# A third quarter of a down projection's columns in seven products of half size

## The chip, the cores and the metric

The kernel runs on one core of a Trainium2 chip. The metric is the device time of one execution in microseconds (us). TensorE (PE) multiplies, VectorE (DVE) and ScalarE (ACT) work elementwise, GpSimd (POOL) and SyncE (SP) here issue transfers: SP the plain loads of weights, POOL the loads that are to be added to what already lies on the chip.

## The reference

A decoder trunk of two layers over 256 tokens and 2048 features, in float32. What the change touches is the MLP, which stands in both layers:

```python
def sq_relu_mlp(u, w_up, w_down):
    hid = jax.nn.relu(u @ w_up)
    return (hid * hid) @ w_down
```

`w_up` is 2048 x 8192, `w_down` 8192 x 2048. Around it stand a mixer (linear attention in layer 0, forgetting attention in layer 1), an embedding gate and norms.

## The kernel before, in words

**Three products for one.** Every float32 weight is split into a high part of reduced precision (`whi`, cast by ACT) and the rest (`wlo`, subtracted by DVE); activations are split the same way. A product is then three matmuls: high x high, high x low, low x high. One split works on 128 x 1024 values and fills one *pair* of buffers (`whi`, `wlo`). There are four pairs, taken in turn, and three `raw` buffers of 128 x 2048 into which SP loads. ACT casts a pair as soon as TensorE has left the pair four before it; DVE follows ACT.

**The MLP.** The 8192 hidden features are worked through in eight blocks of 1024. For block b, eight `up` pieces (128 hidden features each) compute `hid`: weights are the stationary operand, the 256 tokens of `u_m` are streamed, 48 matmuls of 256 columns for two pairs. In between, the pieces of the down projection for block b-1 run with `hid` as the stationary operand (128 tokens) and the weights streamed; they are written out as a list of names that is walked in order (`for item in "up up p1 p2 n0 ..."`). `Line` ties every matmul of the MLP to the one before it, so TensorE runs the pieces exactly in the order of that list. For DVE, ACT and the queues the framework's scheduler chooses the order.

**The down projection before.** The last block (b = 7) goes another way and is not touched. For blocks 0 to 6 of each layer the 2048 output columns are cut in two:

- Columns 0 to 1023 by seven products of half size in place of eight (the scheme of Winograd and Strassen: two halves of the tokens, two of the block's features, two of the columns). The pieces are `p1` to `p7`, 12 matmuls of 512 columns each, in a PSUM bank `pp` that `into` adds to an accumulator `acc1` to `acc7` in SBUF. Five of the seven need sums of weights. They come about in two buffers, `cA` and `cB` (`chain`): POOL loads one quarter of the weights, and once a piece has split it, loads the next quarter with an adding transfer (`accum_op`). The sums of activations (`form`) are made by DVE (line L312).
- Columns 1024 to 2047 plainly, in four pieces `n0` to `n3` of 24 matmuls of 512 columns, which add up over all blocks in four PSUM banks `pn`.

`mm_tokens` (the mixers' values, `pst`) also streams weights past stationary activations: 512 columns in layer 0 (`u_a`), 416 in layer 1 (`u_kv`).

**Where operands start.** Activation buffers start some floats into their tiles: `u_a`, `u_kv` and others at 60 (28 in slot C); `hid` at 36 (4 in slot C), 24 less; weights at 0.

Of the kernel before, what the change touches and what calls it, by code (L numbers as in the profile page):

```python
# [18 lines left out]
P = 128  # L19
# [16 lines left out]
def yoco_kernel(ctx, tc, a, out):  # L36
# [53 lines left out]
    def load_slab(src, n, parts, before=None):  # L90

        raw = wp.tile([P, D], F32, name="raw", tag="raw", bufs=3)
        m = n // parts
        if not before:
            nc.sync.dma_start(raw[:, :n], src)
        got = []
        for i in range(parts):
            r = raw[:, i * m : (i + 1) * m]
            if before:
                before[i]()  # L100
                nc.sync.dma_start(r, src[:, i * m : (i + 1) * m])
            got.append(split(r, m))
        return got

    def split(r, m, to=None, **dims):
        hi = wp.tile([P, 1024], F32R, name="whi", tag="whi", bufs=4)
        lo = wp.tile([P, 1024], F32R, name="wlo", tag="wlo", bufs=4)
        h_, l_ = (x[:, :m].rearrange(to, **dims) if to else x[:, :m] for x in (hi, lo))
        nc.scalar.copy(h_, r)  # L109
        nc.vector.tensor_tensor(l_, r, h_.bitcast(F32), op=ALU.subtract)  # L110
        return hi, lo
# [32 lines left out]
    def mm_tokens(src, act, cols, before=None, after=None):  # L144
# [22 lines left out]
    class Stats:  # L167
# [18 lines left out]
        def rstd(self):  # L186
# [4 lines left out]
            r = base.tile([P, T], F32, name="rstd", tag="rstd", bufs=1)  # L191
# [54 lines left out]
    def mlp(layer, u, stats, slots, u2, g2, pool, pps):  # L246
# [10 lines left out]

        nonlocal h
# [8 lines left out]
        def quarter(b, q, n):  # L267

            return wd[b // 2, b % 2, q, :, 4 * n : 4 * n + 4, :]

        def load(eng, dst, src, **kw):
            eng.dma_start(dst.rearrange("p (n f) -> p n f", n=4), src, **kw)  # L272
        acc = {}
        nsum = None
# [42 lines left out]
        def product(o, op, pairs, start, stop=True):  # L317

            for j in range(4):
                hi, lo = (w[:, j % 2 * 512 : (j % 2 + 1) * 512] for w in pairs[j // 2])  # L320
# [5 lines left out]
        def into(name, ps):  # L326

            if name not in acc:
                acc[name] = pool.tile([P, 512], F32, name="acc" + name, tag="acc" + name, bufs=1)
# [5 lines left out]
        nbank = [[pps.tile([P, 512], F32, name=f"pn{c}{t}", tag=f"pn{c}{t}") for t in range(2)] for c in range(2)]  # L335
# [5 lines left out]

        def loaded(src):
            raw = wp.tile([P, D], F32, name="raw", tag="raw", bufs=3)
# [3 lines left out]
        def down(b):  # L347
# [9 lines left out]
            def one(name, op, pairs):  # L357
                o = psm.tile([P, 512], F32, name="pp", tag="mm")
                product(o, op, pairs, True)
                into(name, o)  # L360

            def p1():
                load(nc.gpsimd, cA, quarter(b, 0, 0))
                pairs = halves(cA)
                load(nc.gpsimd, cA, quarter(b, 0, 1), accum_op=ALU.add)
                one("1", plain(0, 0), pairs)

            def p2():

                load(nc.gpsimd, cB, quarter(b, 1, 1))  # L370
# [7 lines left out]
            def p3():  # L378
                pairs = halves(cB)
                load(nc.gpsimd, cB, quarter(b, 0, 1), accum_op=ALU.add)  # L380
                one("3", form(3), pairs)

            def p6():
                pairs = halves(cA)
                load(nc.gpsimd, cA, quarter(b, 1, 0), accum_op=ALU.add)
                one("6", form(1), pairs)

            def p7():
                one("7", form(2), halves(cB))
# [4 lines left out]
            def n(c, q):  # L394

                pairs = loaded(quarter(b, q, 2 + c))
                for t in range(2):
                    product(nbank[c][t], plain(q, t), pairs, b == q == 0, b == NBL - 2 and q == 1)

            return dict(p1=p1, p2=p2, p3=p3, p4=p4, p5=p5, p6=p6, p7=p7,  # L400
                        n0=lambda: n(0, 0), n1=lambda: n(0, 1), n2=lambda: n(1, 0), n3=lambda: n(1, 1))
# [14 lines left out]
        for to, of, op in ("21+", "61-", "46-", "47-", "56+", "35+", "75+"):  # L416
            nc.vector.tensor_tensor(acc[to], acc[to], acc[of], op=ALU.add if op == "+" else ALU.subtract)
        nsum = pool.tile([P, 4, 512], F32, name="nsum", tag="nsum", bufs=1)
        for i in range(4):
            nc.scalar.copy(nsum[:, i], nbank[i // 2][i % 2])  # L420
        sums = [(acc["2"], acc["4"]), (acc["3"], acc["7"]), (nsum[:, 0], nsum[:, 1]), (nsum[:, 2], nsum[:, 3])]
# [5 lines left out]
        def back(m):  # L427

            for i in range(2):
                n = 4 * m + 2 * i  # L430
                ptr = pps.tile([P, 2, T], F32, name="ptr", tag=f"pn{m % 2}{i}")
                for j in range(2):
                    for t in range(2):
                        nc.tensor.transpose(ptr[:, j, t * P : (t + 1) * P], sums[m][t][:, (n + j) % 4 * P : ((n + j) % 4 + 1) * P], ident)  # L434
# [23 lines left out]
    def ple(layer, u, stats, pt, after, pool, pps):  # L458
# [6 lines left out]
        for n in range(KC):  # L465
            if n % 8 == 0:
                wu = load_slab(a["w_pu"][layer, n // 8], D, 2)
                if n == 0:
                    ups = [two(i) for i in "1562"]
                else:  # L470
                    more = pool.tile([P, 4, 2, T], F32, name="ups", tag="nsum", bufs=1)
                    ups = [more[:, i] for i in range(4)]
                for i in range(4):
                    pu = pps.tile([P, 2, T], F32, name="pu", tag=f"pn{i // 2}{i % 2}")
# [332 lines left out]
    with tc.tile_pool(name="at", bufs=2) as ap, tc.tile_pool(name="aps", bufs=1, space=PSUM) as aps:  # L807
# [30 lines left out]
        nd = ap.tile([NH, T], F32, name="nd", bufs=1)  # L838
# [173 lines left out]
```

## Time and profile before

| | |
|---|---|
| median of 3 runs | 2445.43 us (2445.01 to 2446.1) |
| the profiled execution | 2444.84 us, its span 2443.1 us |
| granted TensorE clock, mean | 0.997 |
| busy: PE / DVE / ACT / POOL | 99% / 72% / 58% / 5% |
| one block of the MLP (640 to 724 us): PE / DVE / ACT busy | 84.0 / 61.5 / 47.1 us |

A matmul's duration in the profile runs to the end of its pipeline, so that neighbours overlap. What one costs in a dense row is the length of the row over its count; the chain in order of time shows such rows.

### The profile page before, as it was taken

How to read it: one execution, taken by the hardware profiler on the slowest of the kernel's cores; microseconds unless marked ns; L12 is line 12 of the kernel's file. 1: busy time of each engine (PE TensorE's matmuls, PEld its weight loads, DVE VectorE, ACT ScalarE, POOL GpSimd, SP SyncE). 2: the span in 40 equal slices, each digit the busy share in tenths (PEclk: the TensorE clock that was granted, in tenths of full speed). 3: DMA queues.
4: the chain of work that ended last, by engine and by line, in shares of the span. 5: the costliest groups of instructions: out<-in, count | busy, mean ns of one | idle time of the engine just before them, and what ended most of it. 6: DMA issues, size and time to landing. Idle time of an engine off the chain costs nothing.

```text
span 2443.1 us, 43577 instructions
## 1 busy us (share of the span) xinstructions
PE 2427.9 (99%) x18024; PEld 2307.7 (94%) x18024; DVE 1765.2 (72%) x2738; ACT 1411.9 (58%) x2112; POOL 119.2 (5%) x159
## 2 busy tenths in 40 slices
PE   9999999999999999999999999999999999999998
PEld 8999999999999999999999999999999999999997
DVE  7797797676777777778874566667677777776876
ACT  7666575565555555555754545556555555555664
POOL 1000000000000000000000000000000000000000
PEclk9999999999999999999999999999999999999999
DMA  6455555578878887876555655557887888778653
GB/s 246 172 182 187 181 174 191 213 259 234 227 234 235 251 237 237 235 223 225 188 178 188 197 177 182 171 196 261 239 231 236 240 245 230 244 231 233 218 190 121
DMA packets 129270, 521.72 MB, mean 214 GB/s; under 512 B 8688, under 2 KB 9264, under 8 KB 91696
## 3 DMA queue, kind: packets, MB, share of 16 engines
q1 hardware_dynamic: 88256, 415.66, 47.8%
q0 software_dynamic: 39520, 101.25, 19.4%
q8 instruction: 141, 2.31, 0.4%
q10 hardware_dynamic: 1296, 2.03, 0.2%
q14 instruction: 57, 0.47, 0.1%
HBM read 512.58 MB, written 6.32 MB: 212 GB/s over the span
## 4 chain that ended last, share of the span: by engine, by line
PE 99%; DVE 0%; ACT 0%; DMA 0%; issue 0%; ACTq 0%; DVEq 0%
PE ps L127 29%; PE pn L127 12%; PE ps L141 12%; PE ps L139 12%; PE ps L140 12%; PE pp L127 11%; PE pst L127 7%; PE pu L141 0%; PE pu L139 0%; PE pu L140 0%; PE pa L671 0%; PE ptr L434 0%; PE pl L874 0%; PE ptp L897 0%; DVE h L945 0%; DMA raw<-in_w_av 0%
## 5 line engine op out<-in xcount | busy, mean ns | idle before, releaser
L110 DVE TENSOR_TENSOR wlo<-raw,whi 128x1024 fp32r<-128x1024 f32 (+2 forms) x798 | 964.8, 1210 | 382.9 <-ACT whi L109 369.8
L109 ACT CAST whi<-raw 128x1024 fp32r<-128x1024 f32 (+2 forms) x798 | 830.8, 1042 | 661.1 <-PE ps L140 281.6
L127 PE MATMUL ps<-u_m,whi 128*128 128x256 f32 x4096 | 701.8, 276 | 0.0
L127 PEld LDWEIGHTS ps<-u_m,whi 128*128 128x128 f32 x4096 | 621.6, 188 | 4.3
L127 PE MATMUL ps<-u_m,wlo 128*128 128x256 f32 x2048 | 564.7, 276 | 0.0
L127 PEld LDWEIGHTS ps<-u_m,wlo 128*128 128x128 f32 x2048 | 384.7, 188 | 0.0
L109 ACT CAST whi<-chain 128x1024 fp32r<-128x1024 f32 x168 | 176.6, 1051 | 215.2 <-PE ps L127 213.3
L110 DVE TENSOR_TENSOR wlo<-chain,whi 128x1024 fp32r<-128x1024 f32 x168 | 205.7, 1225 | 124.6 <-ACT whi L109 123.8
L127 PE MATMUL pn<-whi,hid 128*128 128x512 f32 x896 | 285.1, 389 | 0.0
L127 PE MATMUL pp<-whi,hid 128*128 128x512 f32 x784 | 253.6, 390 | 0.0
L139 PE MATMUL ps<-u_a,whi 128*128 128x256 f32 x768 | 214.0, 279 | 0.0
L141 PE MATMUL ps<-u_a,wlo 128*128 128x256 f32 x768 | 213.3, 278 | 0.0
L140 PE MATMUL ps<-u_a,whi 128*128 128x256 f32 x768 | 212.7, 277 | 0.0
L127 PEld LDWEIGHTS pn<-whi,hid 128*128 128x128 f32 x896 | 168.3, 188 | 34.8
L127 PEld LDWEIGHTS pp<-whi,hid 128*128 128x128 f32 x784 | 147.2, 188 | 29.1
L127 PE MATMUL pn<-wlo,hid 128*128 128x512 f32 x448 | 174.6, 390 | 0.0
L127 PE MATMUL pp<-wlo,hid 128*128 128x512 f32 x392 | 152.9, 390 | 0.0
L272 POOL DMA_DIRECT2D chain<-in_w_down x84 | 93.4, 1112 | 1112.5 <-DVE scr L312 947.6
L139 PEld LDWEIGHTS ps<-u_a,whi 128*128 128x128 f32 x768 | 144.4, 188 | 0.2
L140 PEld LDWEIGHTS ps<-u_a,whi 128*128 128x128 f32 x768 | 144.4, 188 | 0.2
L141 PEld LDWEIGHTS ps<-u_a,wlo 128*128 128x128 f32 x768 | 144.4, 188 | 0.1
L139 PE MATMUL ps<-u_p,whi 128*128 128x256 f32 x512 | 141.4, 276 | 0.0
(287 smaller groups left out, 4476.8 us busy)
## 6 DMA issues: line engine op xcount, KB each, us to landing
raw<-in_w_up SPq DMA_DIRECT2D x128, 1024.0 KB, 5.2
raw<-in_w_down SPq DMA_DIRECT2D x86, 1024.0 KB, 5.3
chain<-in_w_down POOLq DMA_DIRECT2D x84, 1024.0 KB, 8.3
raw<-in_w_ain SPq DMA_DIRECT2D x48, 1024.0 KB, 4.8
raw<-in_w_pg SPq DMA_DIRECT2D x32, 1024.0 KB, 4.8
raw<-in_w_vf SPq DMA_DIRECT2D x20, 832.0 KB, 4.3
raw<-in_w_aout SPq DMA_DIRECT2D x16, 1024.0 KB, 4.9
raw<-in_w_k SPq DMA_DIRECT2D x16, 1024.0 KB, 4.8
```

The source lines that it names most:

```text
L109: nc.scalar.copy(h_, r)
L110: nc.vector.tensor_tensor(l_, r, h_.bitcast(F32), op=ALU.subtract)
L127: ins = nc.tensor.matmul(*args, **kw).ins
L139: mm(ps, wk(pair, kl, 0), act[:, k, 0, :], start=st, stop=False)
L140: mm(ps, wk(pair, kl, 0), act[:, k, 1, :], start=False, stop=False)
L141: mm(ps, wk(pair, kl, 1), act[:, k, 0, :], start=False, stop=sp)
L272: eng.dma_start(dst.rearrange("p (n f) -> p n f", n=4), src, **kw)
```

## The change

Columns 1024 to 1535 also go by seven products now, `q1` to `q7`, on halves of 256 columns: 12 matmuls of 256 columns each, one pair of buffers for a piece. Their weights come in halves of 512 KB. `chq` (a new buffer) and `cq` (the first half of `cB`) hold the sums. `q2`, `q3` and `q4` add up in PSUM (`pq`), the other four in accumulators in SBUF. So that two sums can share a bank, a product with a stationary operand of zeros opens it, once in each layer. Columns 1536 to 2047 stay plain (`n0`, `n1`).

One sum of weights is made by DVE now: `cA += cB` in `p5`, and for the half-size products `chq += cq` in `q3`. `p1`, `p2`, `p3`, `p5`, `p6`, `p7` and `p4` are loaded in another sequence, and the list of pieces is new. The buffers of `whi` and `wlo` are 64 floats longer. The weights of `q` pieces start 32 floats (128 bytes) into them, those of `mm_tokens` with 512 columns 24 floats.

Sums at the end of the layer, transposes, and the buffers that the embedding gate borrows follow from that. Two small tiles share a buffer with another (`rstd`, `nd`).

```diff
-    def split(r, m, to=None, **dims):
-        hi = wp.tile([P, 1024], F32R, name="whi", tag="whi", bufs=4)
-        lo = wp.tile([P, 1024], F32R, name="wlo", tag="wlo", bufs=4)
+    def split(r, m, to=None, shift=0, **dims):
+        hi = wp.tile([P, 1088], F32R, name="whi", tag="whi", bufs=4)[:, shift : shift + 1024]
+        lo = wp.tile([P, 1088], F32R, name="wlo", tag="wlo", bufs=4)[:, shift : shift + 1024]
...
-            pairs = load_slab(src(q), 4 * cols, parts, bef)
+            pairs = load_slab(src(q), 4 * cols, parts, bef, 24 if cols == 512 else 0)
...
+        def whole(r):
+            return [split(r.rearrange("p (n k c) -> p k n c", n=2, k=4), 1024, "p (k n c) -> p k n c", 32, k=4, n=2)]
...
             def p1():
                 load(nc.gpsimd, cA, quarter(b, 0, 0))
+                load(nc.gpsimd, cB, quarter(b, 1, 4))
                 pairs = halves(cA)
-                load(nc.gpsimd, cA, quarter(b, 0, 1), accum_op=ALU.add)
+                load(nc.gpsimd, cA, quarter(b, 0, 4), **add)
                 one("1", plain(0, 0), pairs)
+            def p3():
+                one("3", form(3), halves(cB))
...
             def p5():
-                pairs = halves(cA)
-                load(nc.gpsimd, cA, quarter(b, 1, 1), accum_op=ALU.add)
-                one("5", form(0), pairs)
+                one("5", form(0), halves(cA))
+                for i in range(2):
+                    v, w = (x.rearrange("p (n k c) -> p k n c", n=4, k=4)[:, 2 * i : 2 * i + 2] for x in (cA, cB))
+                    nc.vector.tensor_tensor(v, v, w, op=ALU.add)
+                load(nc.gpsimd, cB, quarter(b, 0, 4), **add)
+            def p7():
+                one("7", form(2), halves(cB))
+                load(nc.gpsimd, cq, quarter(b, 1, 10, 2))
...
+            def q1():
+                load(nc.gpsimd, chq, quarter(b, 0, 8, 2))
+                pairs = whole(chq)
+                load(nc.gpsimd, chq, quarter(b, 0, 10, 2), **add)
+                one("q1", plain(0, 0), pairs)
...
+            def q6():
+                pairs = whole(chq)
+                load(nc.gpsimd, chq, quarter(b, 1, 8, 2), **add)
+                one("q6", form(1), pairs)
+            def q3():
+                product(qbank[0][:, 256:], form(3), whole(cq), False, last)
+                nc.vector.tensor_tensor(chq, chq, cq, op=ALU.add)
+                load(nc.gpsimd, cq, quarter(b, 0, 10, 2), **add)
...
-            for item in "up up p1 p2 n0 up up p5 p3 n1 up up p6 n2 p7 up up p4 n3".split():
+            for item in "up up p1 q1 p3 up p5 n0 q5 p6 up p7 p2 q2 up p4 q3 up q6 up n1 q4 up q7".split():
```

**Where it moves work.** DVE, in the middle of a layer, around `p7`. Before (L110 makes `wlo`, L312 and L315 the sums of activations, L332 adds a bank to its accumulator, L234 writes `hid`): the two halves of `p7`, then `up` pieces.

```order
L110 TENSOR_TENSOR wlo_8981<-chain_6160,whi_8980 128x1024 [waits DMASW3_49,DVE_49,Activation_49]
L312 TENSOR_TENSOR scr_6162<-sqrs_6163,scr_6162 128x128 [waits DVE_49]
L332 TENSOR_TENSOR acc6_7288<-acc6_7288,pp_8932 128x512 [waits PE_49]
L234 TENSOR_TENSOR hid0_3_8363<-sqrs_6163,hid0_3_8363 128x256 [waits Activation_49]
L110 TENSOR_TENSOR wlo_8985<-chain_6160,whi_8984 128x1024 [waits Activation_49]
L312 TENSOR_TENSOR scr_6162<-sqrs_6163,scr_6162 128x128 [waits DVE_49]
L315 TENSOR_TENSOR hid0_3_8363<-scr_6162,hid0_3_8363 128x4x128 [waits Activation_49]
L110 TENSOR_TENSOR wlo_9005<-raw_9002,whi_9004 128x1024 [waits DMAHW3_49,Activation_49]
```

Of the change (L111, L320, L341 and L236 are those lines' new numbers; L444 is `chq += cq`): the second half of `p7`, the two of `p2`, then L444, the one pair of `q2`, and the first of the next `up`.

```order
L111 TENSOR_TENSOR wlo_10706<-chain_6160,whi_10705 128x1024 [waits Activation_49]
L111 TENSOR_TENSOR wlo_10727<-raw_10724,whi_10726 128x1024 [waits DMAHW4_49,PE_49,Activation_49]
L308 SCALAR_TENSOR_TENSOR scr_6165<-ps_10642,rstd_6233 128x256 [waits PE_49]
L111 TENSOR_TENSOR wlo_10731<-raw_10724,whi_10730 128x1024 [waits Activation_49]
L444 TENSOR_TENSOR chq_6161<-chq_6161,chain_6160 128x1024 [waits DMASW2_49]
L320 TENSOR_TENSOR scr_6165<-sqrs_6166 128x128 [waits Activation_49]
L111 TENSOR_TENSOR wlo_10751<-raw_10748,whi_10750 128x1024 [waits DMAHW5_49,DVE_49,Activation_49]
L341 TENSOR_TENSOR acc7_7164<-acc7_7164,pp_10709 128x512 [waits PE_49]
L236 TENSOR_TENSOR hid0_5_10269<-sqrs_6166,hid0_5_10269 128x256 [waits Activation_49]
L320 TENSOR_TENSOR scr_6165<-sqrs_6166,scr_6165 128x128 [waits DVE_49]
L111 TENSOR_TENSOR wlo_10769<-raw_10766,whi_10768 128x1024 [waits DMAHW6_49,Activation_49]
```

The scheduler has put L444, which belongs to `q3`, ahead of the split of `q2`. It waits for the load of `cq`, which is issued once the second half of `p7` is split.

POOL's queue over one block. Before, six loads of 1 MB; the first two fill `cA` and `cB`, the other four add:

```order
L272 DMA chain_6160<-in_w_down 128x4x512 [waits DMASW7_49,DMASW1_49,DVE_49]
L272 DMA chain_6160<-in_w_down 128x4x512 [waits DMASW0_49,DVE_49]
L272 DMA chain_6160<-in_w_down 128x4x512 [waits DMASW2_49,DVE_49]
L272 DMA chain_6160<-in_w_down 128x4x512 [waits DMASW3_49,DVE_49]
L272 DMA chain_6160<-in_w_down 128x4x512 [waits DMASW1_49,DVE_49]
L272 DMA chain_6160<-in_w_down 128x4x512 [waits DMASW4_49,DVE_49]
```

Now five of 1 MB and five of 512 KB (`128x2x512`), shown from the load of `cB` on: `cB`, then adding to `cA`, `chq`, `cB`, `cA`; then `cq`, the next block's `cA`, adding to `cq` and to `chq`, and the next block's `chq`.

```order
L280 DMA chain_6160<-in_w_down 128x4x512 [waits DMASW4_49,DVE_49]
L280 DMA chain_6160<-in_w_down 128x4x512 [waits DMASW3_49,DVE_49]
L280 DMA chq_6161<-in_w_down 128x2x512 [waits DMASW6_49,DVE_49]
L280 DMA chain_6160<-in_w_down 128x4x512 [waits DMASW7_49,DVE_49,Activation_49]
L280 DMA chain_6160<-in_w_down 128x4x512 [waits DMASW0_49,DVE_49]
L280 DMA chain_6160<-in_w_down 128x2x512 [waits DMASW2_49,DVE_49]
L280 DMA chain_6160<-in_w_down 128x4x512 [waits DMASW3_49,DVE_49]
L280 DMA chain_6160<-in_w_down 128x2x512 [waits DMASW4_49,DVE_49]
L280 DMA chq_6161<-in_w_down 128x2x512 [waits DMASW1_49,DVE_49]
L280 DMA chq_6161<-in_w_down 128x2x512 [waits DMASW7_49,DVE_49]
```

Each waits for DVE's split (or addition) of what lies in the buffer; the queue's order is that of these events.

More of the change, by code (lines that the diff above doesn't have):

```diff
@@ L317, in product @@
         def product(o, op, pairs, start, stop=True):
+            m = 4 // len(pairs)
             for j in range(4):
-                hi, lo = (w[:, j % 2 * 512 : (j % 2 + 1) * 512] for w in pairs[j // 2])
+                hi, lo = (w[:, j % m * (1024 // m) : (j % m + 1) * (1024 // m)] for w in pairs[j // m])
                 xh, xl = op(j)
@@ L357, in one @@
             def one(name, op, pairs):
-                o = psm.tile([P, 512], F32, name="pp", tag="mm")
+                w = 1024 // (4 // len(pairs))
+                o = psm.tile([P, w], F32, name="pp", tag="mm")
                 product(o, op, pairs, True)
-                into(name, o)
+                into(name, o, w)
+            last = b == NBL - 2
+            add = dict(accum_op=ALU.add)
             def p1():
                 load(nc.gpsimd, cA, quarter(b, 0, 0))
+                load(nc.gpsimd, cB, quarter(b, 1, 4))
@@ L383, in p6 @@
+            def p7():
+                one("7", form(2), halves(cB))
+                load(nc.gpsimd, cq, quarter(b, 1, 10, 2))
             def p6():
                 pairs = halves(cA)
-                load(nc.gpsimd, cA, quarter(b, 1, 0), accum_op=ALU.add)
+                load(nc.gpsimd, cA, quarter(b, 1, 0), **add)
                 one("6", form(1), pairs)
-            def p7():
-                one("7", form(2), halves(cB))
             def p4():
                 one("4", plain(1, 1), halves(cA))
-            def n(c, q):
-                pairs = loaded(quarter(b, q, 2 + c))
+            def q1():
[3 more added lines that the diff above has]
+                one("q1", plain(0, 0), pairs)
@@ new lines, in q2, with q5 @@
+            def q2():
+                r = raw_tile()[:, :1024]
+                load(nc.sync, r, quarter(b, 1, 8, 2))
+                if b == 0:
+                    pairs = whole(r)
+                    line(qbank[0], zero, pairs[0][0][:, :512], start=True, stop=False)
+                    product(qbank[0][:, :256], plain(1, 0), pairs, False, False)
+                else:
+                    product(qbank[0][:, :256], plain(1, 0), whole(r), False, False)
+            def q5():
+                one("q5", form(0), whole(chq))
@@ new lines, in q6, with q4 @@
+            def q6():
[6 more added lines that the diff above has]
+                load(nc.gpsimd, cq, quarter(b, 0, 10, 2), **add)
+            def q4():
+                product(qbank[1][:, :256], plain(1, 1), whole(chq), b == 0, last)
@@ L397, in n, with q7 @@
+            def q7():
+                one("q7", form(2), whole(cq))
+            def n(q):
+                pairs = loaded(quarter(b, q, 12))
                 for t in range(2):
-                    product(nbank[c][t], plain(q, t), pairs, b == q == 0, b == NBL - 2 and q == 1)
-            return dict(p1=p1, p2=p2, p3=p3, p4=p4, p5=p5, p6=p6, p7=p7,
-                        n0=lambda: n(0, 0), n1=lambda: n(0, 1), n2=lambda: n(1, 0), n3=lambda: n(1, 1))
+                    product(nbank[t], plain(q, t), pairs, b == q == 0, last and q == 1)
@@ L467, in ple @@
                 wu = load_slab(a["w_pu"][layer, n // 8], D, 2)
[L468 to L472, printed above, removed]
+                ups = [two(i) for i in ("1562" if n == 0 else "3156")]
                 for i in range(4):
-                    pu = pps.tile([P, 2, T], F32, name="pu", tag=f"pn{i // 2}{i % 2}")
+                    pu = pps.tile([P, 2, T], F32, name="pu", tag=f"p{'qn'[i // 2]}{i % 2}")
                     for j in range(2):
```

62 lines of the change are left out of this document (37 added, 25 removed).

## The prediction

> **What bounds the kernel now.** The head of the page and the chain that ended last come first.
>
> ```profile
> span 2443.1 us, 43577 instructions
> PE 2427.9 (99%) x18024; PEld 2307.7 (94%) x18024; DVE 1765.2 (72%) x2738; ACT 1411.9 (58%) x2112; POOL 119.2 (5%) x159
> PEclk9999999999999999999999999999999999999999
> PE 99%; DVE 0%; ACT 0%; DMA 0%; issue 0%; ACTq 0%; DVEq 0%
> ```
>
> TensorE runs without a break at full clock, and the chain is TensorE for 99% of the span. What the change does to the time is therefore the matmul time it takes out, less any wait that it makes where there is none now. The chain in order of time gives the price of a matmul: start, length, line and count of dense rows. First the whole span, then 640 to 726 us, one block of layer 0's MLP.
>
> ```profile
> 84.60 20.99 PE pst L127 x90
> 179.54 22.39 PE pst L127 x96
> 275.84 22.39 PE pst L127 x96
> 549.26 10.92 PE ps L127 x96
> 1284.04 72.32 PE pst L127 x384
> ```
>
> ```profile
> 644.74 5.46 PE pp L127 x24
> 650.20 5.44 PE pn L127 x24
> 666.56 2.74 PE pp L127 x12
> 674.74 2.72 PE pp L127 x12
> 696.56 10.92 PE ps L127 x96
> 707.48 5.46 PE pp L127 x24
> 712.94 5.44 PE pn L127 x24
> ```
>
> A plain piece's 512-column matmul costs 5.44/24 = 226.7 ns, a 256-column one of `up` 10.92/96 = 113.75 ns, a 512-column one of layer 0's values (`pst`) 22.39/96 = 233.2 ns. The 416-column ones of layer 1 take 72.32/384 = 188.3 ns. Per column that is 0.443, 0.444, 0.456 and 0.453 ns: two classes. Set beside where the operands start (stationary minus streamed, in floats, whole multiples of 32 dropped), the fast ones have 36 - 0 and 0 - 60, which leave 4, and the slow ones 60 - 0, which leaves 28.
>
> **What the change takes out and adds on TensorE.** Of each block's four plain pieces two go, 48 matmuls of 512 columns, and seven of 12 x 256 columns come, 84. There are seven such blocks in each of two layers, 14 in all.
>
> - Out: 14 x 48 x 226.7 ns = 152.3 us.
> - In: 1176 matmuls of 256 columns whose stationary operand is activations. No row shows that form. The low end is half a plain piece's matmul, 113.3 ns (133.3 us); the high end half of the slow class, 116.6 ns (137.1 us). I take `up`'s 113.75 ns, 133.8 us: the same width, a new stationary operand with every matmul as there, and a start of 36 - 32, which leaves 4 as well.
> - Net: -18.5 us, between -19.0 and -15.2.
>
> The Trainium skill (TensorE: Matmul & The Clock Gate, Back-to-back issue gap) speaks against halving: it gives every warm matmul N/2.4 + 2.5 ns, so 109.2 and 215.8 ns here, and by that the net would be an estimated -16.6 us. This trace has two halves at 227.5 against 226.7 ns, a fixed part of 0.8 ns and not 2.5.
>
> Three small terms. The opening products with zeros are two of 512 columns: +0.45 us. A piece that follows an `up` costs 0.02 us more (2.74 against 2.72, 5.46 against 5.44); the old list has four such places in a block, the new one seven: 14 x 3 x 0.02 = +0.8 us. And `mm_tokens` in layer 0 gets its weights at 24, so 60 - 24 = 36, what the plain pieces have: 6.5 ns less for each of 384 matmuls, of which the first group runs in part at the pace of arriving loads. The bounds are 0 and -2.5; I take -2.2 us, nearest to the dense rows with 282 of them.
>
> **What must stay hidden.** The block's busy times (window, then its length, busy us of each engine, clock, DMA share, GB/s), and DVE's groups in the same 84 us:
>
> ```profile
> 640.00:724.00 84.00, 84.00 (x561) 76.92 (x561) 61.52 (x81) 47.09 (x59) 6.67 (x6) 1.00 0.80 235
> ```
>
> ```profile
> L110 DVE TENSOR_TENSOR wlo<-raw,whi 128x1024 fp32r<-128x1024 f32 x26 | 31.8, 1223 | 8.2 <-ACT whi L109 7.4
> L110 DVE TENSOR_TENSOR wlo<-chain,whi 128x1024 fp32r<-128x1024 f32 x12 | 14.7, 1225 | 9.0 <-ACT whi L109 8.9
> L332 DVE TENSOR_TENSOR acc<-acc,pp 128x512 f32<-128x512 f32 x7 | 4.8, 679 | 0.0
> L234 DVE TENSOR_TENSOR hid<-sqrs,hid 128x256 fp32r<-128x256 f32 x8 | 3.3, 417 | 0.0
> ```
>
> DVE gains three splits (38 become 41), the two halves of `cA += cB` and `chq += cq` (two operands in SBUF of 128 x 1024, as a split has: 1.22 us), six times 1.22 in all, and four additions of 256 columns at about 0.42: +9.0 us, to 70.5 us of a block that shrinks from 84.5 us (eight `up` at 5.46, seven products at 2.73, four plain pieces at 5.44) to 83.2. ACT gains three casts, to some 50. Neither is full, so a wait of TensorE can only come from a run of short pairs. That run has to be followed by hand. DVE's rows from 707 to 716 us (start, length):
>
> ```profile
> 708.48 1.23 DVE L110 TENSOR_TENSOR wlo<-raw,whi 128x1024 fp32r<-128x1024 f32 x1 [0.54 <-ACT whi L109]
> 709.62 0.28 DVE L312 TENSOR_TENSOR scr<-sqrs 128x128 f32<-128x128 f32 x1
> ...
> 711.33 0.68 DVE L332 TENSOR_TENSOR acc<-acc,pp 128x512 f32<-128x512 f32 x1
> 711.92 0.42 DVE L234 TENSOR_TENSOR hid<-sqrs,hid 128x256 fp32r<-128x256 f32 x1
> 712.26 1.22 DVE L110 TENSOR_TENSOR wlo<-raw,whi 128x1024 fp32r<-128x1024 f32 x1
> 713.40 0.28 DVE L312 TENSOR_TENSOR scr<-sqrs,scr 128x128 f32<-128x128 f32 x1
> 713.60 1.22 DVE L110 TENSOR_TENSOR wlo<-raw,whi 128x1024 fp32r<-128x1024 f32 x1
> ```
>
> Back to back, DVE spends 1.14 us on a split (712.26 to 713.40), 0.59 on L332, 0.34 on L234, 0.20 on L312. A pair is ready 2.23 us after TensorE has left the pair four before it (left at 707.48, ready at 708.48 + 1.23). And the cover is thin already: the second half of the plain piece is ready at 713.48 and wanted at 712.94 + 1.36 = 714.30, 0.8 us later, after the four short pairs of `p1 p2`.
>
> The new list has `up p7 p2 q2 up`, five short pairs (1.36 us each) with L444 among them. Let T be the start of `p7`. The pair for the second half of `p2` is free at T, when `up` ends, and DVE starts on it at T + 1.01. Then in the order shown: L444 at T + 2.15, L320 at 3.29, `q2`'s split at 3.49, done at 4.7 (wanted at 5.46), L341, L236 and L320 until 5.76, then the next `up`'s first split, done at 6.98. TensorE wants that at T + 6.82, and its low part one matmul later, 6.93. So the cover is gone there: about 0.05 us too late. I take 0.1 us for each block, +1.4 us; each further 0.1 us of DVE costs the same again.
>
> L444 also waits for the load of `cq`, and DVE takes its instructions in order: behind it stand `q2`'s split, `acc7`, `hid` and the next `up`, and behind these TensorE. The second half of `p7` is split at T - 5.46 + 2.23 = T - 3.23, POOL then issues, so that a landing within 5.4 us of the issue costs nothing. Transfers by POOL, from windows at one issue each and from the page:
>
> ```profile
> chain<-in_w_down POOLq DMA_DIRECT2D x1, 1024.0 KB, 5.6
> ...
> chain<-in_w_down POOLq DMA_DIRECT2D x1, 1024.0 KB, 8.3
> ```
>
> ```profile
> h<-res POOLq DMA_DIRECT2D x2, 2048.0 KB, 8.6
> rb<-hnorm POOLq DMA_DIRECT2D x4, 512.0 KB, 3.9
> ```
>
> A plain load of 1 MB lands after 5.6 us (issued at 600.9 us), an adding one after 8.3 (620.0), 2 MB plain after 8.6. From 5.6 and 8.6, half a megabyte lands after 4.1 us; the other 512 KB transfer took 3.9. I take 4.1: nothing. The bounds are 3.9 and 8.3. The adding loads have more time: the shortest path, `q6` to `q4`, holds `up` and `n1` between, 10.9 us on TensorE.
>
> At no cost: POOL's ten issues for six, under a queue that is busy 6.7 of 84 us; the sums at a layer's end (DVE makes seven more of 256 columns there, ACT two copies fewer): the scheduler has put most of them among the splits of the last block's pieces, and the sums of the half-size products are turned back only after eight products of the last block, 24 matmuls of 113.75 ns or 2.7 us each; 7 x 0.42 = 3 us a layer if that cover were gone. The shared buffers of `rstd` and `nd` are used one after the other in the order of the layers.
>
> **Sum:** -18.5 + 0.45 + 0.8 - 2.2 + 1.4 = -18.0 us. From the execution's 2444.84 us that is 2426.8; the median of the runs shown is 0.6 above that execution, so 2427.4 us.
>
> **The rivals.**
>
> - *DVE stands at L444 because the half-size load is late.* If it lands after x us, each block loses x - 5.4. At the adding loads' 8.3 that is 2.9 x 14 = 41 us, and the kernel takes 2468 us. It decides from x = 6.7, where 14 x 1.3 uses up the gain: slower beyond that. For it: the DMA engines are 80% busy in the block, more bytes are added on the way than before, the scheduler put L444 two splits behind the issue. Against it: both rows at or near this size lie under 4.2.
> - *DVE falls behind by more than the hand count.* Other runs are short of cover too (`p1 q1 p3 up` and `p5 n0`, with 2.4 us of sums). With 0.6 us a block in place of 0.1 the gain is 11 us: 2434.5 us. For it: no cover is left at one place and DVE's idle time falls from 22.5 us in that window to 12.7 a block. Against it: between the runs stand eight `up` pieces and two plain ones in which DVE has time left.
> - *The starts of operands do nothing.* Then `pst` stays at 233.2 and the new matmuls may have the slow class's 116.6: -15.2 + 0.45 + 0.8 + 1.4 = -12.6, 2432.9 us. For it: the two classes could come from something else that `u_a` and `u_kv` share. Against it: four rows of three widths fall in line. The Trainium skill (SBUF — State Buffer, Who interferes with whom) is on this rival's side: TensorE has a read port for each operand and waits for no one, so where they start should not matter. The difference between 233.2 and 226.7 ns at one shape does not agree with it.
>
> **How the numbers follow.** Forecast 0.68, late load 0.07, DVE behind 0.15, starts without effect 0.10. A difference of under 0.2%, 4.9 us, cannot be told from none. The forecast, the third rival and nearly all of the second lie below 2440.5 us, and so does the first while x stays under 6.3: faster 0.90, same 0.03, slower 0.07. The forecast's own span is from -20.2 us (no wait, half a plain matmul, all of `pst`) to about -15. The range runs from 2424.5 to 2437.5: it holds the third rival and most of the second, and leaves out the first.
>
> **What would show it.** In the changed kernel's chain: `pn` rows of 24 once where two stood, 12 new matmuls in 1.36 to 1.37 us (1.40 in the slow class), `pst` rows of 96 in 21.8 us. In the waits: TensorE for DVE (`wlo`) a few us in all, at the `up` after `q2`; DVE L444 for the load of `cq` next to nothing. The prediction is wrong if TensorE's waits sum to over 10 us, if the new matmuls cost over 117 ns, or if a 512 KB load by POOL takes over 5.4 us.

## The result, and the profile after

The changed kernel takes 2487.95 us (median of 4 runs, 2486.08 to 2489.39) where the kernel before takes 2445.58 in the same session: a ratio of 1.0174, with a 95% interval of 1.0162 to 1.0187. It is 42 us slower. The prediction was 2427.4 us and 18 us faster, with 0.07 on slower.

The head of the page and its chain, of the kernel after the change:

```profile
span 2487.7 us, 44964 instructions
PE 2440.3 (98%) x18530; PEld 2340.6 (94%) x18530; DVE 1865.5 (75%) x2886; ACT 1446.7 (58%) x2158; POOL 173.1 (7%) x215
PE 80%; DMA 8%; issue 7%; DVE 3%; ACT 1%; ACTq 0%; DVEq 0%; POOLq 0%
```

TensorE was 99% of the chain, now it is 80%: transfers and DVE stand in it. The page's line below names the transfer: `DMA chain<-in_w_down` has 8% of the span. The waits of the whole run (who waited, at which line, for whom; us in total, times, the longest) show the same thing in three rows of 14 waits each, the last two with one for each block:

```profile
ACT whi L110 <- DMA chain<-in_w_down: 36.1, 14, 3.8
DVE chq L444 <- DMA chain<-in_w_down: 36.0, 14, 3.5
PEld pq L128 <- DVE wlo L111: 35.7, 14, 3.2
```

One block of it, as the chain from 715 to 762 us (start, length, what):

```profile
727.37 11.02 DMA chain<-in_w_down
...
738.49 1.06 ACT whi L110
...
741.39 1.15 DVE wlo L111
...
742.83 4.52 DMA chain<-in_w_down
...
747.37 0.07 DVE chq L444
...
748.79 1.15 DVE wlo L111
...
749.98 2.09 PE pq L128 x11
752.07 6.65 PE ps L128 x48
```

Read it downwards. The load that adds to `cB` is issued at 727.37 and lands 11.0 us later; ACT has been waiting for it to split `p7`. DVE finishes the second half of that split at 742.53, POOL then issues the load of `cq`, which lands at 747.34; L444 has been waiting for that. Behind L444 comes `q2`'s split, and TensorE gets on with `q2` (`pq`) at 749.98. The `up` that follows takes 6.65 us where 5.46 were usual, though DVE hardly holds it back. Two windows of 2 us of that `up` show why (window, its length, busy us of PE, PEld, DVE, ACT and POOL, granted clock, DMA share, GB/s):

```profile
752.00:754.00 2.00, 2.00 (x11) 1.95 (x10) 2.00 (x4) 1.05 (x1) 0.00 (x0) 0.50 0.95 401
756.00:758.00 2.00, 2.00 (x20) 2.00 (x20) 1.96 (x3) 1.01 (x1) 0.80 (x1) 1.00 0.93 347
```

In the first the granted clock is 0.50 and TensorE has 11 matmuls in hand, in the second 1.00 and 20; by their ends they follow one another in 213 and 113 ns. Such a stretch at half clock, 3.4 us long, stands behind 10 of the 14 waits at `pq`, and nowhere else between the first 30 and the last 15 us of the run. In the kernel before there is none in that time. These stretches account for the mean granted clock of 0.991, which was 0.997 before. Which waits bring one on is not settled: by the matmuls' ends the ten that are followed by one are 2.2 to 3.3 us long, the four others 0.8 to 2.8.

TensorE's time has gone up in three places. By the ends of all its matmuls, the 504 of `pq` lost 40 us, 35.6 in waits and some 4.6 at half clock. The 6144 of `up` took 715.0 us instead of 698.7: some 3 us of that are waits, 8 half clock, and 4 a price of 114.3 ns for 113.7. The third place is the new products themselves. Two chain rows of the same run, one new piece each (start, length, count of matmuls):

```profile
673.64 1.42 PE pq L128 x12
680.57 1.43 PE pp L128 x12
```

And the chain's rows of layer 0's values, the second, third and fourth of four groups:

```profile
85.35 21.00 PE pst L128 x90
180.28 21.77 PE pst L128 x96
275.94 21.77 PE pst L128 x96
```

A new matmul costs 118 to 119 ns and not 113.75, 5.9 us over 98 pieces of 12. The values take 21.77 us in two groups, as forecast (21.8), and 21.00/90 = 233.3 ns, as before, in the one ahead of them. All of it together (40 + 16 + 6 + 2, less the 2.2 us that the forecast had for the first two) is 62 us. The profiled execution, 2489.39 us, lies 62.6 us above the 2426.8 that the forecast has for one execution, the median 60.6 above its 2427.4.

### The profile page after: what moved, and what is told of

Its sections match the earlier page's. It is cut to its first block, busy times and chain, and to the rows that moved or that the text cites. A ratio compares the mean times of both kernels' runs of the same rounds, so it can differ in the third digit from the quotient of the medians.

```text
span 2487.7 us, 44964 instructions
## 1 busy us (share of the span) xinstructions
PE 2440.3 (98%) x18530; PEld 2340.6 (94%) x18530; DVE 1865.5 (75%) x2886; ACT 1446.7 (58%) x2158; POOL 173.1 (7%) x215
## 4 chain that ended last, share of the span: by engine, by line
PE 80%; DMA 8%; issue 7%; DVE 3%; ACT 1%; ACTq 0%; DVEq 0%; POOLq 0%
PE ps L128 23%; PE ps L140 12%; PE ps L141 12%; PE ps L142 12%; DMA chain<-in_w_down 8%; PE pst L128 7%; PE pp L128 5%; PE pn L128 4%; PE pq L128 2%; DVE wlo L111 2%; ACT whi L110 1%; DVE acc L341 0%; PE pu L140 0%; PE pu L142 0%; PE pu L141 0%
## 5 line engine op out<-in xcount | busy, mean ns | idle before, releaser
L110 ACT CAST whi<-raw 128x1024 fp32r<-128x1024 f32 (+2 forms) x756 | 785.3, 1041 | 682.1 <-PE ps L141 288.7
L111 DVE TENSOR_TENSOR wlo<-raw,whi 128x1024 fp32r<-128x1024 f32 (+2 forms) x756 | 912.1, 1208 | 355.4 <-ACT whi L110 348.7
L128 PE MATMUL pp<-whi,hid 128*128 128x512 f32 (+1 forms) x1232 | 338.2, 351 | 0.0
L110 ACT CAST whi<-chain 128x1024 fp32r<-128x1024 f32 x196 | 204.6, 1050 | 199.9 <-PE ps L128 72.5
L111 DVE TENSOR_TENSOR wlo<-chain,whi 128x1024 fp32r<-128x1024 f32 x196 | 238.2, 1222 | 78.7 <-ACT whi L110 75.8
L128 PEld LDWEIGHTS pp<-whi,hid 128*128 128x128 f32 x1232 | 217.9, 188 | 29.6
L128 PE MATMUL pp<-wlo,hid 128*128 128x512 f32 (+1 forms) x616 | 216.0, 351 | 0.0
L128 PE MATMUL pn<-whi,hid 128*128 128x512 f32 x448 | 142.6, 389 | 0.0
L140 PE MATMUL ps<-u_p,whi 128*128 128x256 f32 x512 | 141.2, 276 | 0.0
L142 PE MATMUL ps<-u_p,wlo 128*128 128x256 f32 x512 | 140.9, 275 | 0.0
L141 PE MATMUL ps<-u_p,whi 128*128 128x256 f32 x512 | 140.9, 275 | 0.0
```

Of the source, the lines that this page charges most:

```text
L128: ins = nc.tensor.matmul(*args, **kw).ins
L140: mm(ps, wk(pair, kl, 0), act[:, k, 0, :], start=st, stop=False)
L141: mm(ps, wk(pair, kl, 0), act[:, k, 1, :], start=False, stop=False)
L142: mm(ps, wk(pair, kl, 1), act[:, k, 0, :], start=False, stop=sp)
```

## The experiments

All times stand beside runs of the kernel before on the same chip. "Behind" in the diffs is a scheduling edge without a semaphore: the instruction gets its place behind another of its own engine. Around it the scheduler also moves a few small instructions of DVE (L320, L323) by a place or two; their number and kind stay. `ends` lists the low-part instructions of the splits in the order of the program.

| kernel | us | ratio to before, 95% | DVE's wait at L444 | wait for `pq`'s weights | load to `cB`, median us | load of `cq`, median us | stretches at half clock |
|---|---|---|---|---|---|---|---|
| after | 2487.95 | 1.0174 (1.0162 to 1.0187) | 36.0 | 35.7 | 10.8 | 5.5 | 10 |
| add_later | 2437.94 | 0.9973 (0.9963 to 0.9982) | none | 0.8 | 10.7 | 5.5 | none |
| plain_p7 | 2476.34 | 1.013 (1.011 to 1.015) | 34.1 | 27.4 | 5.5 | 7.4 | 5 |
| no_p4load | 2462.80 | 1.0075 (1.0055 to 1.0095) | 18.2 | 18.6 | 10.7 | 4.1 | 1 |
| both_gone | 2437.55 | 0.9970 (0.9957 to 0.9984) | none | none | 5.5 | 4.0 | none |
| cq_sp | 2487.27 | 1.0175 (1.0155 to 1.0195) | 35.6 | 36.4 | 10.8 | 5.5 | 9 |
| add_mid | 2468.83 | 1.0098 (1.0083 to 1.0113) | 15.3 | none; `ps` 25.4 | 10.7 | 5.5 | 6 |
| starts | 2438.38 | one execution | none | | | | none |
| no_starts | 2438.00 | 0.9975 (0.9964 to 0.9985) | none | | | | none |
| hid_60 | 2446.5 | one execution | none | | | | none |
| order_b | 2434.86 | 0.9960 (0.9946 to 0.9974) | none | none | | | none |
| order_e | 2456.23 | 1.0047 (1.0032 to 1.0062) | none | | | | 1 |
| like_up | 2445.99 | 1.0007 (0.9998 to 1.0017) | none | none | | | none |

Waits are us in all, of the profiled execution; the last column counts as above. Cells that no argument needs are empty.

### L444 out of the way: add_later

```diff
-                nc.vector.tensor_tensor(chq, chq, cq, op=ALU.add)
+                behind(nc.vector.tensor_tensor(chq, chq, cq, op=ALU.add).ins, ends[-1])
```

`ends[-1]` is the split of `q3`, which needs `cq` anyway. No work is left out.

> The changed kernel with one instruction of DVE moved: chq += cq (L444) is put behind the split of q3 instead of ahead of q2's. Theory (DVE stands at L444 until the load of cq lands, and q2's split stands behind it): in the changed kernel DVE waited 36.0 us at L444 and TensorE about 40 us at pq and 13 us inside up. With the add out of the way the waits at pq go to under 3 us in all and most of those in up too, so 2488 - 40 = 2448 us at most and 2488 - 53 = 2435 us at best. Rival (the load before it, of cB, is what is late: ACT waited 36.1 us for it at p7's cast): then the wait only moves to p7's products (pp), and the time stays above 2470 us.

One instruction in each block moved by six splits, and 50 us are gone: 2437.94 us, 7 us faster than before the change. DVE's rows of the same block (start, length; a wait would stand in brackets at the row's end) show `q2`'s split at 739.76 at once, and L444 at 749.12 without a wait:

```profile
739.76 1.23 DVE L111 TENSOR_TENSOR wlo<-raw,whi 128x1024 fp32r<-128x1024 f32 x1
...
749.12 1.22 DVE L444 TENSOR_TENSOR chq<-chq,chain 128x1024 f32<-128x1024 f32 x1
```

The loads are as slow as they were. So it is the place of L444 in DVE's order that turns a late load into 50 us of TensorE's time: waits at `pq`, and the half clock behind them, which is most of the 13 us that the expectation above takes for waits inside `up`. The rival (TensorE would wait at `p7` instead) falls. ACT still waits as long for the loads to `chain`, and no piece waits for ACT:

```profile
ACT whi L110 <- DMA chain<-in_w_down: 40.9, 20, 3.8
```

The Trainium skill (PSUM — Partial Sum Buffer, Engine vs sequencer instructions) calls VectorE's queue a strict FIFO; the two orders of the same instructions agree with that.

### L444 moved by one split: add_mid

```diff
-                nc.vector.tensor_tensor(chq, chq, cq, op=ALU.add)
+                behind(nc.vector.tensor_tensor(chq, chq, cq, op=ALU.add).ins, ends[-6])
```

> The changed kernel with L444 moved by one split: behind q2's split, ahead of the two of the next up. Theory (everything that stands behind L444 on DVE pays): TensorE's waits at pq go, but the next up now waits for its first split instead: the load of cq lands at the same time, L444 ends 1.2 us after that, then 0.7 us of small work and a split of 1.2 us, about 1.8 us after TensorE wants it; 14 x 1.8 = 25 us in place of the 53 us of the changed kernel: 2455 to 2466 us. Rival (only the order of L444 and q2's split matters, since only the short piece has no cover): as fast as with L444 behind q3's split, 2436 to 2441 us.

2468.83 us, a little above the range named, with the waits where they were expected and as long (25 us); behind six of them comes a stretch at half clock, which the range did not have. The waits of this run:

```profile
PEld ps L128 <- DVE wlo L111: 25.4, 13, 2.9
DVE chq L444 <- DMA chain<-in_w_down: 15.3, 12, 2.0
```

`pq` waits no more, the next `up` does. Each split that stands behind a waiting instruction pays for it, not only the short piece's.

### Why the load of cq lands so late: plain_p7, no_p4load, both_gone, cq_sp

First the load to `cB` that `p7` waits for, made a plain one (the addition is left out):

```diff
-                load(nc.gpsimd, cB, quarter(b, 0, 4), **add)
+                load(nc.gpsimd, cB, quarter(b, 0, 4))
```

> The changed kernel, with the load that adds block column 4 of the first half to cB (for p7) made a plain one. It leaves that addition out, so one of the seven products of the outputs is wrong; everything else, the order of DVE too, is the same. Theory (the chain p5, L402, adding load of cB, p7's split, load of cq, L444 is too long by about 2.6 us a block, of which the adding load's 10.8 us are the largest part): the plain load lands in 5.5 to 7.5 us, ACT's 36 us of waiting at p7 and DVE's 36 us at L444 both go to under 5 us, and the time to 2435 to 2450 us. Rival (L444 waits because the load of cq is itself too slow, whatever stands before it): the wait at L444 stays over 20 us and the time over 2465 us.

Half of it came: the load lands after 5.5 us, ACT's wait for `chain` falls from 36.1 to 3.8 us. But the time falls by 12 us only, because the load of `cq`, issued earlier, now takes 7.4 us in the median. The rival's prediction (over 20 us of waiting, over 2465 us) is met, though not its reason. The landings told what holds it: in the changed kernel and in this one the load of `cq` landed 1.2 to 2.8 us after the 1 MB adding load that POOL issues at `p6` for `p4`, in all 28 blocks. That load was taken away next (its addition is left out), with L444 held at the place it has in the changed kernel:

```diff
-                load(nc.gpsimd, cA, quarter(b, 1, 0), **add)
```

> The changed kernel without the adding load of 1 MB to cA that POOL issues at p6 for p4 (the addition is left out, so one of the seven products of the outputs is wrong); the order of DVE's instructions is the same, L444 stands where it stood. Theory (one queue: POOL's loads land in the order of their issue, and the load of cq, issued 8 to 9 us after that adding load, cannot land before it; in the changed kernel it landed 1.24 to 2.60 us after it in all 14 blocks): the load of cq lands 3.9 to 4.5 us after its issue in every block (median 5.5 before), the load of cB before it comes faster too (10.8 before, 8.3 to 10 now), L444 waits under 10 us in all (36.0) and the time is 2440 to 2455 us. Rival (transfers of SP at the same time are what slow the loads): the load of cB stays at 10.5 to 11, that of cq gains at most half a microsecond, L444 still waits over 25 us and the time is over 2470 us.

The row of the load in a window of 6 us around it (738 to 744):

```profile
chain<-in_w_down POOLq DMA_DIRECT2D x1, 512.0 KB, 4.1
```

And the same run's waits at the two places:

```profile
PEld pq L128 <- DVE wlo L111: 18.6, 12, 2.3
DVE chq L444 <- DMA chain<-in_w_down: 18.2, 11, 2.0
```

The load of `cq` lands after 4.0 to 4.5 us in every block, as forecast for it alone. The load to `cB` stays at 10.7, as the rival had it, and the time lies between the two: 2462.80 us. Each of the two accounts for a part, so both were taken away, with the two edits above:

> The changed kernel with both taken away: the load to cB before p7 made a plain one, and p4's adding load to cA left out (two additions are missing, so two of the seven products of the outputs are wrong). L444 stands where the change put it. Theory (the load of cq is late because the two adding loads ahead of it fill the DMA engines and POOL's queue; nothing else is wrong with L444's place): p7's split is done about 4 us earlier, the load of cq lands 4.0 to 4.5 us after its issue, L444 waits under 5 us in all, TensorE under 5 us at pq, and the time is that of the kernel with L444 moved: 2436 to 2444 us. Rival (DVE has too much work at this place, L444's own 1.2 us ahead of q2's split being part of it): L444's wait is gone, TensorE still waits over 10 us at pq and ps, and the time is over 2448 us.

2437.55 us, the time of the kernel with L444 moved, with L444 where the change put it. The chain is TensorE alone again:

```profile
span 2435.7 us, 44922 instructions
PE 99%; DVE 0%; ACT 0%; DMA 0%; issue 0%; ACTq 0%; DVEq 0%
```

So the place of L444 does harm only through the two late loads, and DVE has no lack of time there: its 1.2 us ahead of `q2`'s split is covered. Last, the load of `cq` on another queue:

```diff
-                load(nc.gpsimd, cq, quarter(b, 1, 10, 2))
+                load(nc.sync, cq, quarter(b, 1, 10, 2))
```

> The changed kernel with the plain load of cq issued by SP and not by POOL, nothing left out; DVE's order is the same. Theory (one queue): the load of cq no longer lands behind p4's adding load but 4 to 5 us after its issue; the load of cB, which is 10.8 us late as before, still holds p7's split back. In the changed kernel its landings took 4.4 to 7.0 us, mean 5.4, so at 4.0 the gain is 1.4 us a block or 20 us: 2465 to 2472 us. Rival (the queue plays no part, transfers share the DMA engines): the load of cq takes as long as before, and SP's loads of weights, which now stand behind it, are later: 2485 us or more.

Nothing: 2487.27 us, and a landing of 5.5 us in the median as on POOL's queue; from SP's queue, too, the load lands 0.9 to 2.6 us behind `p4`'s in all 14 blocks. My theory that POOL's order of landing was what held it falls. What fits is that the DMA engines themselves are full. Windows of the changed kernel, first the block, then the time from the issue of the load to `cB` to the landing of `cq` (after the window and its length: busy us of PE, PEld, DVE, ACT and POOL, clock, DMA share, GB/s):

```profile
640.00:727.00 87.00, 84.16 (x595) 78.83 (x594) 67.35 (x90) 49.11 (x61) 9.54 (x10) 0.98 0.82 230
727.37:747.34 19.97, 19.97 (x120) 17.67 (x118) 13.82 (x16) 12.25 (x15) 3.30 (x3) 1.00 0.94 222
```

Below, from its view of transfers, the queues of POOL (q0) and SP (q1) from 727 to 739 us: packets, MB, share of the 16 engines.

```profile
q0 software_dynamic: 676, 1.35, 66.4%
q1 hardware_dynamic: 272, 0.52, 15.9%
```

For those 20 us the engines are 94% busy. POOL's queue, in these 12 us adding loads alone, takes 0.664 x 16 x 12 / 1.35 = 94 us of engine time for a megabyte, SP's plain loads 0.159 x 16 x 12 / 0.52 = 59. Here an adding megabyte takes 1.6 times a plain one. From 615 to 632 us of the kernel before, with one adding load in all, the same working gives 0.358 x 16 x 17 / 1.05 = 93 us for it and 0.438 x 16 x 17 / 2.61 = 46 for SP's: the ratio is 2 where less runs side by side. The change puts two adding megabytes ahead of `cq`'s load. The one to `cB` has landed when it is issued; `p4`'s, issued at 734.1, lands at 746.1 and runs beside it. The Trainium skill (DMA: Bandwidth & Descriptors, Issuing engines are not separate DMA queues) says that transfers started by different engines run on the same 16 DMA engines and interleave, so that another issuer saves the issue alone; by that the move to SP should gain nothing, and the run agrees: 5.5 us on either. Why the load to `cB` takes 10.7 us, also without `p4`'s beside it, where an adding megabyte took 8.3 in the prediction's row, was not tried by itself; SP moves half a megabyte beside it, which itself takes 8.0 us.

### What sets the price of a matmul: starts, no_starts, hid_60, like_up

On top of add_later, each half-size piece gets its own start as a second argument of `whole`, and the values' four slabs theirs:

```diff
-            pairs = load_slab(src(q), 4 * cols, parts, bef, 24 if cols == 512 else 0)
+            pairs = load_slab(src(q), 4 * cols, parts, bef, (0, 28, 56, 24)[q] if cols == 512 else 0)
-                one("q5", form(0), whole(chq))
+                one("q5", form(0), whole(chq, 8))
```

> The kernel with the add moved, and the splits of the seven half-size pieces written at seven different starts: q1 at 0, q2 at 4, q5 at 8, q6 at 16, q7 at 24, q3 at 36, q4 at 60 floats; and the four slabs of the first layer's values at 0, 28, 56 and 24. Stationary operands start at 36 (pieces) and 60 (values), as before. The difference theory (stationary less streamed, whole 32s dropped; 4 is fast): q1 (4) takes 12 x 113.5 = 1.36 us, the others (0, 28, 20, 12, 0, 8) up to 1.42; values at 56 and 24 (both 4) are equal and below those at 0 (28). Rival A (a half-size product with activations as stationary operand costs 118.7 ns wherever its weights start): all seven take 1.42 us. Rival B (the start of the streamed operand alone counts): q1 at 0 is fast like the full pieces, which stream from 0, and the values at 0 are no slower than the rest.

One execution took 2438.38 us. Its chain rows, the pieces being `q2` (4), `q3` (36), `q6` (16), `q4` (60) and `q7` (24):

```profile
658.31 1.40 PE pq L128 x12
...
667.96 1.44 PE pq L128 x12
674.91 1.41 PE pp L128 x12
...
687.25 1.43 PE pq L128 x12
694.16 1.42 PE pp L128 x12
```

1.40 to 1.44 us; `q1` at 0 and `q5` at 8, from their matmuls' ends, 118 and 119 ns each. No start gives 113.75. The four mixed starts of the values gave 22.34 us a group, no better than 22.39 at 0. One of the four is the 24 that the change gives to every slab: there two groups run at 227 ns, here that slab takes 233 in each group, by its matmuls' ends. So where a matmul's own two operands start does not settle its price. Rival A stands. Undoing the starts altogether:

```diff
-        pairs = load_slab(src(q), 4 * cols, parts, bef, 24 if cols == 512 else 0)
+        pairs = load_slab(src(q), 4 * cols, parts, bef, 0)
-        return [split(..., 32, k=4, n=2)]
+        return [split(..., 0, k=4, n=2)]
```

> The kernel with L444 behind q3's split, and all splits back at the start of their buffers (0 in place of 32 for the half-size pieces and of 24 for the first layer's values), the buffers as long as in the changed kernel. Theory (the starts buy next to nothing: seven different starts gave the half-size products 117 to 120 ns): half-size products 118 to 119 ns, values 233 ns for 230, so +0.0 to +2 us against the kernel with the starts: 2437 to 2441 us. Rival (the difference of starts sets the class; at 0 and 36 the difference is 4 as at 32 and 36, but the values fall back): only the values change, +1.2 us. Second rival (32 is better than 0 for reasons not seen): half-size products over 121 ns, 2441 us or more.

2438.00 against 2437.94 us: the starts are worth nothing that can be measured. The values are back at 22.39 us a group and the full pieces of 512 columns (`pp`) at 229.5 ns for 228.1 (their own start, 0, is the same in both), so the starts do win there; they lose as much in `up` (114.3 ns with them, 113.9 without) and in the half-size pieces (118.7 and 118.0).

The stationary operands of all pieces at 60 in place of 36, on top of add_later:

```diff
-                f = slot_flat(slots[b % 2], f"hid{layer}_{b}", 0 if b == NBL - 1 else 24)
+                f = slot_flat(slots[b % 2], f"hid{layer}_{b}", 0)
```

> The kernel with L444 moved, and the stationary operands of all pieces starting at 60 floats in place of 36; the streamed weights as in the change, at 0 for full pieces and at 32 for half-size ones. Difference rule of the prediction (stationary less streamed; 4 fast, 28 slow): full pieces 28, so pn goes from 227 to 233 ns a matmul and the time up by about 1300 x 6.5 ns = 8 us or more; half-size products 60 - 32 = 28 too, so no faster than 118.7. Rival (where the stationary operand starts plays no part): pn 227, half-size 118.7, the time 2438 us.

One execution took 2446.5 us. The chain rows of `q3` and `n1` in add_later, with 36:

```profile
667.39 1.42 PE pq L128 x12
681.26 5.46 PE pn L128 x24
```

And in this kernel, with 60:

```profile
667.80 1.44 PE pq L128 x12
681.60 5.63 PE pn L128 x24
```

Full pieces go from 227 to 234 ns, as the difference rule says; half-size ones stay at 118 to 120. Then the pair of starts that `up` has, with the difference 4 that the rule calls fast, on top of order_b (below):

```diff
-                f = slot_flat(slots[b % 2], f"hid{layer}_{b}", 0 if b == NBL - 1 else 24)
+                f = slot_flat(slots[b % 2], f"hid{layer}_{b}", 0 if b == NBL - 1 else 28)
```

and 60 for the start of all pieces' weights.

> The kernel with L444 behind q3's split and the list of the run before that gave 2434.86 us, with both operands of all pieces at the starts that up has: the stationary one at a multiple of 32 floats (36 becomes 32), the weights that are streamed at 60 (full pieces from 0, half-size ones from 32). Difference rule: 32 - 60 leaves 4, the fast class. Theory 1 (the pair of starts sets the class, and 0 and 60 is the pair with which up takes 113.7 ns): the half-size products fall from 118.7 to about 114 ns, 1176 x 4.7 = 5.5 us, full pieces stay at 227: 2429 to 2431 us. Theory 2 (a 256-column product whose stationary operand is the activations costs 118 to 120 ns wherever its operands start; only 512-column ones have two classes): full pieces 227, half-size 118 to 120: 2434 to 2436 us. Rival (nothing but 36 and 0 is fast for the full pieces): pn at 230 ns or more, 2438 us or more.

Its chain rows of the same two pieces:

```profile
673.80 1.41 PE pq L128 x12
682.10 5.66 PE pn L128 x24
```

With the difference 32 - 60, which leaves 4, the full pieces take 5.66/24 = 236 ns, the slowest seen, and 11 us are lost. The difference rule falls with it. The half-size pieces take 117 ns, 1 to 2 below what they cost elsewhere. What makes a 256-column product with activations in the array 118 ns, where `up`'s with weights in it takes 114, stays open: no start tried brings it there.

### Another list of pieces: order_b, order_e

Both keep L444 behind `q3`'s split. order_b is `up up p1 q1 p3 up p5 n0 q5 p6 up up p7 p2 q2 up p4 q3 q6 up n1 up q4 q7`.

> The kernel with L444 behind q3's split, and another list: up up p1 q1 p3 up p5 n0 q5 p6 up up p7 p2 q2 up p4 q3 q6 up n1 up q4 q7. There are six places where a piece follows an up, in place of seven, and p7 has one more up ahead of it. Theory (each change from up to pieces and back costs up some 0.05 us: 5.51 for 5.46 us): 14 x 0.07 = 1 us less, and the few waits of up that are left (about 3 us) go: 2434 to 2437 us. Rival (q3 and q6 now stand next to each other, so q6's split waits for L444 behind a load of cq that is late): TensorE waits at q6, 2442 us or more.

2434.86 us, 0.9960 of before (0.9946 to 0.9974) and the fastest here. TensorE is 99% of its chain, `up` takes 114.09 ns a matmul for 114.3 in the changed kernel without its waits, and the late sum moves where nobody waits behind it: ACT waits 35.1 us for L444 at `q6`'s split, and TensorE not at all.

> The kernel with L444 behind q3's split and the list: up up p1 q1 p3 up up p5 n0 q5 p6 up p2 q2 up p7 p4 up q3 q6 n1 up q4 q7. Six places where a piece follows an up; p7 stands 5.5 us later, behind q2, so no piece with cover too short stands behind its late load; q3 an up behind it. Theory: no wait of DVE for a load anywhere ahead of work that TensorE wants; 2434 to 2437 us. Rival (the chains q6, load, q4 and p7, load, q3 are now the short ones): ACT or DVE wait there for the loads and TensorE with them, 2442 us or more.

2456.23 us, slower. Its chain shows a wait that neither theory named:

```profile
650.60 1.15 DVE wlo L111
651.76 8.72 DMA raw<-in_w_up
...
660.58 1.06 ACT whi L110
661.66 1.24 DVE wlo L111
...
662.94 5.55 PE ps L128 x46
```

The load of weights for an `up` starts only when DVE's split has freed its buffer, and takes 8.72 us; the `up` behind `p2 q2` waits for it.

## Why the prediction was wrong, step by step

- **The wait at L444: the step that failed.** It said that "a landing within 5.4 us of the issue costs nothing" and took 4.1 us. The 5.4 came from a split of `p7` done at T - 3.23, T being the start of `p7`, by the rule that a pair is split as soon as TensorE frees it. But `p7`'s split also waits for the load to `cB`. In the block above, `p7` can start at T = 742.31 (the `up` ahead of it starts at 736.85 in TensorE's timeline and takes 5.46), and its second half is split at 742.53, T + 0.2, 3.4 us after the time assumed. From there the prediction's own hand count holds: L444 starts at T + 5.1 for T + 2.15, 2.9 us late, `q2`'s split is done that much later, and TensorE, which wants it at T + 5.46, waits 2.1 us there. Then it runs at half clock for 3.4 us, up to 1.7 us more; the prediction priced a wait at its length alone. The 4.1 us for the landing was right for a load alone (4.0 to 4.5 in no_p4load) and 1.4 too low beside `p4`'s load.
- **Where the time of the loads was judged.** "The adding loads have more time: the shortest path, `q6` to `q4`" named the wrong path. The short one runs from `p5` over the sum on chip (L402) and the load to `cB` to `p7`'s split and the load of `cq`; the prediction never followed it, since no row of before has the sum in it. The row with 80% DMA share was read as an average: in the 20 us that matter it is 94%.
- **The rival that came true.** "DVE stands at L444" had the mechanism, with the condition wrong: it needed no landing over 6.7 us, since it is the issue that comes 3.4 us late. That its 41 us are near the 40 lost at `pq` is luck: they stand for a landing of 8.3 us, and its formula, x - 5.4, gives 1.4 us in all for the 5.5 measured. A chance of 0.07 for it was far too small: the argument looked only at how long the load takes, never at when it can be issued.
- **DVE's own amount of work**: small, as it said. both_gone has no wait at `pq` with L444 ahead of `q2`, so the cover of 0.05 us too little, +1.4 us, cost nothing that shows; the rival "DVE behind" has nothing for it.
- **The new products**: mis-sized. 118.7 ns measured for 113.75, outside the bounds of 113.3 to 116.6, so the swap of pieces gains 18.5 - 5.9 = 12.6 us. The bounds came from halves of 512-column rows and from one 256-column form with the operands in the other roles.
- **The starts**: the values' two groups at 21.77 are right, the rule behind it is not: one group stays at 233.3 ns with the same starts, and a difference of 4 gave 236 ns in like_up. The third rival's 116.6 was too low too, though its claim, that starts do nothing for the new products, is the one that held.
- **Small terms**: a change from `up` to a piece and back costs more than 0.02 us. `up` rows of 5.48 to 5.51 us for 5.46 make 112 of them some 4 us longer in add_later. The profiled execution of add_later, 2440.3 us, lies 13.5 us above the 2426.8 forecast for one. Of these the new products are 6.5 (0.7 of it waits), the values 1.6, `up` 6.3 (705.0 us for 698.7, 2.2 of it waits that order_b no longer has) and the full pieces 0.8, less the 2.2 forecast for changes and cover: 13.0, which leaves 0.5 us unexplained.

## What to carry to other kernels

Before a wait on an engine's queue is priced at nothing, follow what it waits for back to an event whose time a row shows, through every transfer and split on the way; two links that are each a little late add up, and either one hides the other (12 and 25 us singly, 50 together). A wait of TensorE can cost more than its length, where the clock falls behind it. Put an instruction that waits for a transfer behind all the work on its engine that does not, by an explicit edge where a scheduler places by estimated times: here one edge was worth 50 us. And take the DMA share from the very stretch in which the transfer runs, with its adding loads weighed by their engine time, not their bytes.

## What the runs showed of the hardware

A 256-column product with activations as the stationary operand took 117 to 120 ns at eight starts of the streamed operand and three of the stationary one; the same width with weights stationary took 113.7. With 512 columns the price went with the starts from 227 ns at 36 and 0 (stationary, streamed) to 234 at 60 and 0 and 236 at 32 and 60; but values at 60 and 24 took 227 ns in two groups and 233 in another, so the two starts alone do not set it. An adding load kept the DMA engines busy 1.6 times as long per megabyte as plain ones in the same 12 us (94 against 59 us), and twice as long in a stretch with less beside it (93 against 46). A half-megabyte plain load took 4.0 to 4.1 us (median) with no adding load beside it and 5.5 with one, on POOL's queue as on SP's. Behind 10 of 14 waits of TensorE of 0.8 to 3.3 us the granted clock fell to 0.50 for 3.4 us, and 256-column matmuls followed one another in 213 ns for 113.
